# One rate in a planner's estimate: loads and stores taken to follow each other at the closer spacing throughout

## The chip, the cores and the metric

The kernel runs on one core of a Trainium2 chip. The metric is the device time of one execution in microseconds, here the median of three runs. TensorE (PE) multiplies matrices, with weight loads (PEld) beside it; VectorE (DVE), ScalarE (ACT) and GpSimd (POOL) do the rest, and SyncE (SP) issues nearly all DMAs. Each engine works through its own instructions in the order in which the program has them, and waits on semaphores for the others.

## The reference

One inference step of a two-layer streaming encoder, for a prompt of 2048 frames and a running stream of 32 frames, model width 1024, all in float32. Layer 0 is sliding-window attention (16 heads of 64, ALiBi, sinks), layer 1 a gated DeltaNet (8 heads of 128), each with a SiLU gate, a residual add and RMSNorm around it:

```
hp = rmsnorm(xp, norm_g[i]);  hs = rmsnorm(xs, norm_g[i])
layer 0: q, k, v, gate = split(h @ w_in);  o = sink_attention(q, k, v)
         y = (o * silu(gate)) @ w_out
layer 1: qkv, z, b, a = split(h @ w_in);   qkv = silu(causal_conv(qkv))
         o, s = gated_delta_chunked(l2norm(q), l2norm(k), v, g, beta, s0, 64)
         y = (rmsnorm(o) * silu(z)) @ w_out
xp = xp + yp;  xs = xs + ys
y_prompt = rmsnorm(xp, final_norm_g);  y_sample = rmsnorm(xs, final_norm_g)
```

Also returned are the newest K/V rows, the last rows before the convolution and the delta-rule states.

## The kernel before

**Tiles and stages.** Activations lie with features on the 128 partitions. The tokens are cut into four slabs of 512 (`SLABS`); the 32 sample frames ride on slab 1, which is therefore 544 wide and is multiplied in two groups of 272 columns. The attention layer runs over the four slabs, then the DeltaNet layer over the four slabs. Per slab a layer is a row of *blocks*: one block is one 1024x128 piece of a weight matrix against the slab. An attention slab has 20 input blocks and 8 output blocks (`wa`, `wao`), a delta slab 33 and 8 (`wd`, `wdo`).

**A block.** Each weight is split into a high and a low float32r part (tiles `wh`), and so are the activations (`hk`); a block is 8 x 3 matmuls (high by high, high by low, low by high) into one PSUM bank. Banks for blocks (`pj`) are two, used in turn (`BANKS`), so the bank of one block must have been emptied before the block after the next can start. In an output block (`out_blocks`) the emptying is one DVE addition, `xr <- pj, xr`, which adds the residual; ACT then squares it (`sq`), DVE sums the squares (`acc`), and a DMA stores it (`xsx1`).

**Weights.** In the attention layer a weight half of 256 KB is loaded to `wr` (3 buffers), ACT casts it to the high part (`wh <- wr`) and DVE subtracts to get the low part (`wh <- wr, wh`). There are 6 `wh` buffers; a block uses 4. Meanwhile `keep_ahead` does the same splitting for all 41 weights of the DeltaNet layer, in 82 halves, and writes the parts to DRAM: load `pr` (2 buffers), ACT cast `ph <- pr` (1 buffer), store, DVE subtraction `pr <- pr, ph`, store. The DeltaNet layer then loads its `wh` ready split (`wh <- xswwd`).

**Order.** The program is first generated in one order (classes `Kern`, `Estimate`) and only recorded. `Order.flush` then plans it anew, once after the attention layer and once at the end: a list scheduler that, with estimated durations, always takes the instruction that can start first, by rank among those ready on an engine. What it emits is the order in which each engine has to work. All instructions are recorded through one helper, so that every row of the profile has line L185. The planner counts DMAs on one shared channel, in ns:

```
self.free[e] = now + 60
self.dma = max(now + 1500, self.dma) + op.cost * (self.CLOSE if now < self.START else 1)
op.ends = {"dma": self.dma + 500}
```

`op.cost` is bytes / 250, thus 1049 for 256 KB. `CLOSE` is 0.7, which makes it 734 for 256 KB (250 and 357 bytes per ns). `START` is 25000: by the planner's own clock, the first 25 us. What needs a load, or the buffer of a store, can't stand in the order ahead of what the planner thinks starts before that DMA has landed.

Of the kernel before, what the change touches and what calls it, by code (L numbers as in the profile page):

```python
# [211 lines left out]
class Order:  # L212
# [2 lines left out]

    ENGINES = ("tensor", "vector", "scalar", "gpsimd", "sync")

    START, EARLY, CLOSE = 25000, 5000, 0.7

    EVAC, CHAIN = 400, 600  # L220
# [92 lines left out]
    def flush(self):  # L313

        overs = []
        for p in self.places.values():
            if p.old and p.over is None:
                p.over = Op(None)
                overs.append(p.over)
                for o in p.old.ops:  # L320
                    self.link(o, p.over)
                for o in {id(o): o for o in p.ops}.values():
                    self.link(p.over, o)
                    if o.gang:
                        self.link(p.over, o.gang)
        self.wait = {e: [] for e in self.ENGINES}
        ready = {e: [] for e in self.ENGINES}
        for o in [o for o in overs + self.ops if o.left == 0]:
            self.settle(o)
        while any(self.wait.values()) or any(ready.values()):  # L330
            when = {e: max(self.free[e], 0.0 if ready[e] else self.wait[e][0][0]) for e in self.ENGINES if ready[e] or self.wait[e]}
            e = min(when, key=when.get)
            now = when[e]
            while self.wait[e] and self.wait[e][0][0] <= now:
                _, rank, o = heapq.heappop(self.wait[e])
                heapq.heappush(ready[e], (rank, o))
            _, op = heapq.heappop(ready[e])
            op.call()
            if op.dma:
                self.free[e] = now + 60  # L340
                self.dma = max(now + 1500, self.dma) + op.cost * (self.CLOSE if now < self.START else 1)
                op.ends = {"dma": self.dma + 500}
            else:
                self.free[e] = now + op.cost
                op.ends = {e: self.free[e]}
            op.start = now
            self.finish(op)
        assert all(o.done for o in self.ops)
        self.ops = []
# [1903 lines left out]
```

## Time and profile before

| | |
|---|---|
| runs | 2346.01, 2347.42, 2352.44 us; median 2347.42 |
| profiled execution | 2349.7 us, of which span of the core 2347.9 us |
| PE busy | 2243.8 us (96%), weight loads 1842.6 (78%) |
| DVE, ACT, POOL busy | 1724.0 (73%), 1262.7 (54%), 467.8 (20%) |
| mean granted clock of PE | 0.98 |
| DMA | 382.75 MB, mean 163 GB/s |

The attention layer takes the first 915 us or so, the DeltaNet layer the rest; the splitting ahead ends at about 617 us. PE is busy nearly all the time; it is idle for 104 us in all, and its clock is at half in some stretches.

### The profile page before, as it was taken

The page shows a single profiled execution, that of the slowest core. Times are in us where ns is not written, and L with a number is a line of the kernel's source. Part 1 is how long each engine was busy: PE and PEld are TensorE (multiplying, and loading weights), DVE is VectorE, ACT ScalarE, POOL GpSimd, SP SyncE. Part 2 cuts the span into 40 slices and gives each one's busy share as a digit, 9 for nine tenths or more (in the row PEclk, how much of TensorE's full clock was granted, in tenths as well). Part 3 has the DMA queues.
Part 4 walks back from the last instruction along what each step waited for, and adds up shares of the span by engine and source line. Part 5 has one row for each costly group of instructions (what it writes and reads, how often), then busy time and mean ns, then how long its engine had stood idle before and what let it go on. Part 6 is the DMA issues. An engine that isn't in the chain of part 4 may idle for free.

```text
span 2347.9 us, 44428 instructions
## 1 busy us (share of the span) xinstructions
PE 2243.8 (96%) x14759; PEld 1842.6 (78%) x14759; DVE 1724.0 (73%) x5330; ACT 1262.7 (54%) x3792; POOL 467.8 (20%) x738
## 2 busy tenths in 40 slices
PE   8999999989999999999999999989999999999997
PEld 6777899877777777777788788867798777777776
DVE  7785667757665565688987677888886888786876
ACT  6664566546554553556566355465644465535533
POOL 0120000301110001222233031231313222122222
PEclk9999999999999999999999999999999999999998
DMA  8567655765443226544533673433457634476442
GB/s 272 190 203 231 219 187 183 222 220 193 153 138 112 66 64 203 180 133 127 173 95 112 207 240 102 133 115 125 149 177 226 188 117 137 139 225 206 153 139 68
DMA packets 222832, 382.75 MB, mean 163 GB/s; under 512 B 29922, under 2 KB 45194, under 8 KB 222602
## 3 DMA queue, kind: packets, MB, share of 16 engines
q1 hardware_dynamic: 220154, 377.75, 50.4%
q8 instruction: 116, 1.90, 0.3%
q10 hardware_dynamic: 2448, 2.16, 0.3%
q14 instruction: 114, 0.93, 0.1%
HBM read 311.63 MB, written 68.19 MB: 162 GB/s over the span
## 4 chain that ended last, share of the span: by engine, by line
PE 66%; DVE 22%; ACT 6%; issue 3%; DMA 1%; POOL 1%; SPq 0%; DVEq 0%; ACTq 0%; POOLq 0%
PE pj L185 47%; PE tb L185 7%; PE ta L185 6%; PE tc L185 4%; DVE cy L185 4%; DVE sub L185 3%; DVE tl L185 3%; ACT ta L185 2%; DVE ml L185 1%; DVE md L185 1%; DVE r L185 1%; PE ms L185 1%; ACT kd L185 1%; DVE st L185 1%; DVE kq L185 1%
## 5 line engine op out<-in xcount | busy, mean ns | idle before, releaser
L185 PE MATMUL pj<-hk,wh 128*128 128x512 f32 (+1 forms) x8184 | 1770.5, 363 | 34.0 <-DVE xr L185 16.3
L185 PEld LDWEIGHTS pj<-hk,wh 128*128 128x128 f32 x8184 | 1326.5, 191 | 246.4 <-issue 29.2
L185 DVE SCALAR_TENSOR_TENSOR cy<-cx,cw,cy 128x512 f32<-128x512 f32 x360 | 230.5, 651 | 45.7 <-ACT cy L185 40.9
L185 DVE TENSOR_TENSOR wh<-wr,wh 128x512 fp32r<-128x512 f32 x224 | 159.1, 712 | 139.5 <-ACT wh L185 129.4
L185 ACT CAST wh<-wr 128x512 fp32r<-128x512 f32 x224 | 138.0, 618 | 203.2 <-PE pj L185 174.0
L185 ACT ACTIVATE qs<-tb,egq 64x128 f32<-64x128 f32 x264 | 95.7, 362 | 90.5 <-DVE r L185 79.6
L185 POOL TENSOR_TENSOR hk<-of,hk 128x256 fp32r<-128x256 f32 (+1 forms) x72 | 53.4, 742 | 444.8 <-ACT hk L185 439.2
L185 ACT ACTIVATE s<-s,mx 128x256 f32<-128x256 f32 (+1 forms) x272 | 132.0, 487 | 7.5 <-DVE mx L185 7.2
L185 DVE TENSOR_TENSOR sub<-ml,tl 128x60 f32<-128x60 f32 (+24 forms) x527 | 125.8, 239 | 10.2
L185 ACT ACTIVATE cx<-cy 128x512 f32<-128x512 f32 (+1 forms) x96 | 61.1, 636 | 130.4 <-DVE cy L185 95.7
L185 DVE TENSOR_TENSOR tl<-tl,sub 128x60 f32<-128x60 f32 (+24 forms) x527 | 123.0, 233 | 10.1
L185 DVE CUSTOM_DVE_ANT_0 s<-ta,bias 128x256 f32<-128x256 f32 (+1 forms) x272 | 96.2, 404 | 25.6 <-PE ta L185 25.5
L185 DVE SCALAR_TENSOR_TENSOR r<-tb,nbk,vb 64x128 f32<-64x128 f32 x264 | 91.7, 348 | 29.8 <-PE tb L185 25.3
L185 ACT ACTIVATE qs<-o 128x128 f32<-128x128 f32 x132 | 40.7, 308 | 132.2 <-DVE o L185 126.8
L185 ACT COPY cx<-pj 128x512 f32<-128x512 f32 (+2 forms) x149 | 64.1, 445 | 77.8 <-PE pj L185 66.0
L185 PE MATMUL tb<-st,kq 128*128 128x128 f32 x512 | 95.0, 287 | 5.5 <-DVE st L185 5.0
L185 PEld LDWEIGHTS tb<-st,kq 128*128 128x128 f32 x512 | 82.7, 194 | 20.4 <-DVE st L185 12.3
L185 DVE SCALAR_TENSOR_TENSOR st<-st,egl,tc 128x128 f32<-128x128 f32 x128 | 44.3, 346 | 59.4 <-PE tc L185 56.9
L185 ACT COPY pt<-tb 128x512 f32<-128x512 f32 (+2 forms) x144 | 70.6, 528 | 26.4 <-PE tb L185 26.1
L185 DVE TENSOR_SCALAR s<-s,den 128x256 f32<-128x256 f32 (+1 forms) x272 | 81.7, 352 | 1.1
L185 PE MATMUL tc<-pt,vt 128*64 128x128 f32 (+2 forms) x1056 | 79.7, 279 | 1.1 <-DVE of L185 0.6
L185 POOL TENSOR_TENSOR so<-so,mhalf 128x4 f32<-128x4 f32 x33 | 36.8, 1114 | 216.4 <-DVE so L185 188.6
(242 smaller groups left out, 3447.8 us busy)
## 6 DMA issues: line engine op xcount, KB each, us to landing
wh<-xswwd SPq DMA_DIRECT2D x528, 256.0 KB, 2.9
wr<-in_wa SPq DMA_DIRECT2D x160, 256.0 KB, 3.3
wh<-xswwdo SPq DMA_DIRECT2D x112, 256.0 KB, 3.0
pr<-in_wd SPq DMA_DIRECT2D x66, 256.0 KB, 3.4
xswwd<-ph SPq DMA_DIRECT2D x66, 256.0 KB, 3.6
xswwd<-pr SPq DMA_DIRECT2D x66, 256.0 KB, 3.0
wr<-in_wao SPq DMA_DIRECT2D x64, 256.0 KB, 2.9
xa<-in_x SPq DMA_DIRECT2D x48, 256.0 KB, 4.0
```

The source lines that it names most:

```text
L185: self.order.add(Op(self.name, lambda: call(*args, **kw), cost, op == "dma_start"), ins, outs)
```

## The change

The planner's factor `CLOSE` holds for all DMAs and no more for those of the first 25 us alone. Nothing else changes: the same instructions with the same operands and buffers are recorded in the same order, and what the planner makes of them differs.

```
-                self.dma = max(now + 1500, self.dma) + op.cost * (self.CLOSE if now < self.START else 1)
+                self.dma = max(now + 1500, self.dma) + op.cost * self.CLOSE
```

The number `START` stays in use in `Order.add`, unchanged. The emitted order changes soon after the first blocks. On PE, ACT and DVE it is the same, or nearly, from where the splitting ahead ends to the end of the attention layer, and on all engines in the last delta slab.

DVE in the output blocks of slab 0 of the attention layer, before (`xr` empties the bank of a block, `wh` is a low weight part, `pr` a low part of the splitting ahead; the last number of a name counts tiles in the order of generation):

```order
L185 TENSOR_TENSOR wh_546_682<-wr_538_672,wh_545_681 128x512
L185 TENSOR_TENSOR xr_520_652<-pj_532_664,xr_520_652 128x512
L185 TENSOR_TENSOR acc_522_654<-acc_522_654,sq_542_676 128x512
L185 TENSOR_TENSOR wh_548_684<-wr_539_673,wh_547_683 128x512
L185 TENSOR_TENSOR pr_646_796<-pr_646_796,ph_680_832 128x512
L185 TENSOR_TENSOR wh_557_695<-wr_549_685,wh_556_694 128x512
L185 TENSOR_TENSOR wh_559_697<-wr_550_686,wh_558_696 128x512
L185 TENSOR_TENSOR xr_531_663<-pj_541_675,xr_531_663 128x512
```

The same place now:

```order
L185 TENSOR_TENSOR xr_520_652<-pj_532_664,xr_520_652 128x512
L185 TENSOR_TENSOR wh_546_682<-wr_538_672,wh_545_681 128x512
L185 TENSOR_TENSOR acc_522_654<-acc_522_654,sq_542_676 128x512
L185 TENSOR_TENSOR wh_548_684<-wr_539_673,wh_547_683 128x512
L185 TENSOR_TENSOR pr_797_957<-pr_797_957,ph_822_984 128x512
L185 TENSOR_TENSOR xr_531_663<-pj_541_675,xr_531_663 128x512
L185 TENSOR_TENSOR wh_557_695<-wr_549_685,wh_556_694 128x512
```

The emptying `xr_531` stood behind the low parts 557 and 559 and now stands ahead of both; and the splitting ahead, which had its tile `pr_646` here, has its tile `pr_797`.

DVE in the output blocks of slab 1 (two groups of 272 columns, so two emptyings a block), before:

```order
L185 TENSOR_TENSOR wh_1202_1396<-wr_1192_1385,wh_1201_1395 128x512
L185 TENSOR_TENSOR wh_1210_1406<-wr_1203_1397,wh_1209_1405 128x512
L185 TENSOR_TENSOR xr_1181_1373<-pj_1194_1387,xr_1181_1373 128x272
L185 TENSOR_TENSOR xr_1181_1373<-pj_1197_1391,xr_1181_1373 128x272
L185 TENSOR_TENSOR acc_1161_1351<-acc_1161_1351,sq_1207_1402 128x544
```

and now:

```order
L185 TENSOR_TENSOR xr_1181_1373<-pj_1194_1387,xr_1181_1373 128x272
L185 TENSOR_TENSOR wh_1202_1396<-wr_1192_1385,wh_1201_1395 128x512
L185 TENSOR_TENSOR xr_1181_1373<-pj_1197_1391,xr_1181_1373 128x272
L185 TENSOR_TENSOR wh_1210_1406<-wr_1203_1397,wh_1209_1405 128x512
L185 TENSOR_TENSOR pr_1715_1959<-pr_1715_1959,ph_1727_1973 128x512
```

Each emptying has moved ahead of the low part that it stood behind.

PE in delta slab 1 (`ta <- tq, mo` is a small product of the inverse, which waits for DVE; `pj` are blocks), before:

```order
L185 MATMUL pj_3449_12439<-hk_2881_11871,wh_3415_12405 128x272
L185 MATMUL pj_3449_12439<-hk_2881_11871,wh_3416_12406 128x272
L185 MATMUL pj_3449_12439<-hk_2884_11874,wh_3415_12405 128x272 x2
L185 MATMUL ta_3436_12426<-tq_3425_12415,mo_3321_12311 32x32
L185 MATMUL ta_3437_12427<-tq_3425_12415,mo_3321_12311 32x32
```

and now:

```order
L185 MATMUL pj_3469_12459<-hk_2884_11874,wh_3432_12422 128x272 x2
L185 MATMUL pj_3469_12459<-hk_2884_11874,wh_3433_12423 128x272
L185 MATMUL pj_3469_12459<-hk_2892_11882,wh_3452_12442 128x272 x2
L185 MATMUL ta_3436_12426<-tq_3425_12415,mo_3321_12311 32x32
L185 MATMUL ta_3437_12427<-tq_3425_12415,mo_3321_12311 32x32
```

The small products stand one block later: behind the second group of the block that follows.

## Rows read from the trace of the kernel before

**Rows 1.** The page: the span, and the busy time of PE.

```profile
span 2347.9 us, 44428 instructions
PE 2243.8 (96%) x14759; PEld 1842.6 (78%) x14759; DVE 1724.0 (73%) x5330; ACT 1262.7 (54%) x3792; POOL 467.8 (20%) x738
```

**Rows 2.** Windows by stage: PE, PEld, DVE, ACT, POOL busy; PE clock; DMA share; GB/s.

```profile
25.00:620.00 595.00, 574.40 (x4051) 483.67 (x4049) 411.88 (x1269) 348.34 (x933) 72.21 (x83) 0.99 0.64 208
620.00:915.00 295.00, 292.62 (x1714) 226.72 (x1714) 181.10 (x538) 152.47 (x397) 29.44 (x33) 1.00 0.33 105
915.00:1990.00 1075.00, 1027.85 (x6997) 858.10 (x6996) 851.18 (x2712) 582.34 (x1912) 280.70 (x495) 0.98 0.49 154
1990.00:2348.00 358.00, 330.58 (x1935) 259.69 (x1933) 264.79 (x789) 164.40 (x529) 83.63 (x120) 0.94 0.49 156
```

**Rows 3.** Waits of PE from 25 to 650 us: total us, times, longest.

```profile
PE pj L185 <- DVE xr L185: 15.9, 9, 1.9
PE pj L185 <- ACT hk L185: 1.8, 2, 1.6
```

**Rows 4.** Timeline of DVE, output blocks of slab 0: start, duration, idle before.

```profile
199.25 0.69 DVE L185 TENSOR_TENSOR xr<-pj,xr 128x512 f32<-128x512 f32 x1 [1.65 <-PE pj L185]
199.85 0.68 DVE L185 TENSOR_TENSOR wh<-wr,wh 128x512 fp32r<-128x512 f32 x1
...
204.79 0.69 DVE L185 TENSOR_TENSOR xr<-pj,xr 128x512 f32<-128x512 f32 x1 [1.67 <-PE pj L185]
```

**Rows 5.** Timeline of all engines, some blocks later.

```profile
226.79 0.62 ACT L185 CAST wh<-wr 128x512 fp32r<-128x512 f32 x1 [1.87 <-PE pj L185]
227.44 0.69 DVE L185 TENSOR_TENSOR wh<-wr,wh 128x512 fp32r<-128x512 f32 x1 [1.80 <-ACT wh L185]
228.05 0.68 DVE L185 TENSOR_TENSOR xr<-pj,xr 128x512 f32<-128x512 f32 x1
...
228.88 5.84 PE L185 MATMUL pj<-hk,wh 128*128 128x512 f32 x24 [1.94 <-DVE xr L185]
...
235.82 0.68 DVE L185 TENSOR_TENSOR xr<-pj,xr 128x512 f32<-128x512 f32 x1
```

**Rows 6.** Timeline of PE in the output blocks of slab 1.

```profile
475.31 6.22 PE L185 MATMUL pj<-hk,wh 128*128 128x272 f32 x48 [1.80 <-DVE xr L185]
```

**Rows 7.** Windows, PE alone: busy, clock, DMA share, GB/s.

```profile
196.00:227.00 31.00, 30.94 (x134) 1.00 0.82 273
227.00:248.00 21.00, 15.30 (x65) 0.92 0.65 203
238.00:241.40 3.40, 3.40 (x10) 0.50 0.62 204
465.00:505.00 40.00, 31.02 (x207) 0.91 0.68 220
484.00:497.40 13.40, 11.60 (x69) 0.75 0.70 225
```

**Rows 8.** DMA issues from 25 to 300 us: count, KB each, median us to landing.

```profile
wr<-in_wa SPq DMA_DIRECT2D x51, 256.0 KB, 3.7
...
pr<-in_wd SPq DMA_DIRECT2D x36, 256.0 KB, 3.3
xa<-in_x SPq DMA_DIRECT2D x26, 256.0 KB, 4.7
```

**Rows 9.** DMA issues of the whole run, from the page.

```profile
wh<-xswwd SPq DMA_DIRECT2D x528, 256.0 KB, 2.9
```

**Rows 10.** The splitting's DVE work (`pr`) in a window: busy, clock, share, GB/s.

```profile
25.00:620.00 595.00, 58.29 (x82) 0.99 0.64 208
```

**Rows 11.** Waits for DMAs from 25 to 650 us, the one of ACT on the splitting.

```profile
ACT ph L185 <- DMA xswwd<-ph: 2.1, 3, 1.3
```

**Rows 12.** Waits of PE from 915 us to the end.

```profile
PE tb L185 <- DVE r L185: 13.5, 12, 3.8
PE ta L185 <- DVE tq L185: 7.0, 10, 2.1
```

## Prediction

> **What bounds the kernel now.** I read the page first. PE is busy for 2243.8 of 2347.9 us [rows 1], so the kernel is bound by TensorE, and a new order can only move the other 104 us and the stretches at half clock. The windows by stage say where these are [rows 2]: 20.6 us idle from 25 to 620 us (595.00 - 574.40), 2.4 us from 620 to 915, 47.2 us from 915 to 1990 and 27.4 us in the last slab and the end. The stage from 25 to 620 us is the one in which the weights of the second layer are split ahead; there the DMA share is 0.64, and right behind it, with that work done, 0.33.
>
> Next the waits of PE in that stage [rows 3]: of its idle time 15.9 us, in nine waits of up to 1.9 us, ended with the DVE addition `xr`, which empties a block's bank. Nothing else there comes near: the next is 1.8 us. The timeline shows what it is. Early in slab 0's output blocks an `xr` runs at 199.25 and the next at 204.79 us, each directly after its block ended, with a low weight part behind it [rows 4]; a block takes 5.54 us and PE is busy 30.94 of 31 us [rows 7]. Some blocks later `xr` stands behind a low part that itself waited 1.80 us for ACT; it starts at 228.05, PE gets its bank only then and sits idle for 1.94 us [rows 5]; the next `xr` follows at 235.82, so that a block takes 7.77 us. DVE was not short of time (busy for 411.88 of 595 us [rows 2]), it had an instruction in front that was waiting. Slab 1 has the same, 1.80 us before a block of 6.22 us [rows 6].
>
> The planner put it there. It counts 1049 ns on one channel for each 256 KB, 250 GB/s; the stage moves 208 on average and 273 in the output blocks [rows 2, 7], so in its books the channel is full, loads land late, and what hangs on them slides behind what does not. The chip was not late: the cast in that place waits for PE to free a buffer (at 226.79 [rows 5]), and ACT waited for the splitting's stores only 2.1 us in all [rows 11].
>
> **The change, part by part.** No instruction is added or removed; every edit is a move.
>
> *The emptyings move ahead of the low parts (slabs 0 and 1).* The order quoted for the change has in every output block of both slabs the pattern of the early blocks of slab 0, one emptying ahead of the low parts. Nine waits, 15.9 us, go [rows 3]. What would be late next is the weight part that now runs behind `xr`, 0.69 us later; in the blocks from 196 to 227 us it stood so, and PE lost 0.06 us in 31 [rows 7]. So I take -15.9, with 0 as the other end if the bank is late for another reason.
>
> *The clock.* The granted clock was 1.00 (2.4 GHz) from 196 to 227 us and 0.50 (1.2 GHz) from 238.0 to 241.4, amid three of these waits (PE busy 15.30 of 21 us from 227 to 248); from 484.0 to 497.4 it was 0.75 on average, again amid them [rows 7]. At half clock half the work is lost: 3.4 x 0.50 = 1.7 us and 13.4 x 0.25 = 3.4 us, together 5.1. Without the waits I take these as gone: -5.1, bounds -5.1 and 0.
>
> *The splitting ahead runs earlier.* Its 82 halves, 58.29 us of DVE [rows 10] and as many casts, are the same work in other places; in the output blocks of slab 0 DVE is then five halves further on (tile 797 for 646). It is hidden under PE as before, since DVE and ACT are busy 69% and 59% of the stage. Its price is the DMA queue. One output block of slab 0 with one half in it moves 7 transfers of 256 KB (two weight halves, residual in, sum out, one load and two stores of the splitting), 1.835 MB, at 5.54 us 331 GB/s. The row from 196 to 227 us gives 273 GB/s at a share of 0.82 [rows 7], 333 at a full share: with nine halves in eight blocks, 15.5 MB, it takes 46.5 us for 44.3 us of PE work, 2.2 us over. For the loads of the next slab's statistics, which land after 4.7 us at this load where weights take 3.7 [rows 8], I add a like amount, as they stand ahead of other work on ACT and DVE. I take +5 in all. The bounds are 0 (at a share of 0.82 PE lost nothing [rows 7]) and +21 (the queue gives all of the gain back).
> The Trainium skill (DMA: Bandwidth & Descriptors, Specifications) puts the limit of memory for one core at about 358 GB/s, almost the planner's new 357; by that, 331 fits and the 2.2 us fall away, which would make the sum 2 us less. The trace of this case has no stretch above the 333 worked out here, so the measured one decides.
>
> *The DeltaNet layer.* Weight loads there land after 2.9 us [rows 9], between the 2.73 us (1500 + 734 + 500) that the planner will now count for a transfer alone and the 3.05 (1500 + 1049 + 500) that it counted. Blocks move forward on PE and the small products of inverse and chain backward, by up to one block, as in the place quoted, where PE then has 6 us more work (a block of 48 matmuls [rows 6]) in front of a product that waited for DVE. Such waits are the largest there: 13.5 us for `r`, 7.0 for `tq` [rows 12]. But a chain that runs later is later for its own next step too, and at the end of the slab it is work that stands alone. No row tells the sign. I take 0, bounds -15 and +15, a third of the 47 us idle from 915 to 1990 us [rows 2].
>
> *The sum* for the profiled execution, 2349.7 us with 1.8 us around the span: 2349.7 - 15.9 - 5.1 + 5 = 2333.7. The median of the runs is 2.3 us lower (2347.42), so I forecast 2332 there (2331.4, rounded up).
>
> **The rivals.**
> *The queue sets the pace (slower).* The splitting's cast `ph` has one buffer, so it waits for its own store, and ACT waits with it, in order; behind it stand the casts of the weights PE needs. Before, the planner's late landings kept these apart (2.1 us of such waits [rows 11]). If the landings rise by a microsecond, as from the 3.7 of weights to the 4.7 of `xa` [rows 8], each of 82 halves can hold ACT for 1 us; with a third of it reaching PE, since ACT is 59% busy [rows 2], that is +27, against which perhaps 15 of the 21 us remain: 2347.4 + 12 = 2359. It decides once the DMA share from 25 us to the splitting's end comes near the 0.82 that only the output blocks have now. Against it: at 0.82 PE lost nothing [rows 7].
> The Trainium skill (DMA: Bandwidth & Descriptors, Latency and other measured facts) has the latency of memory go from 0.2 us on average to 2 us at high load, which speaks for this rival. In this trace a transfer's landing grew from 2.9 to 3.7 and 4.7 us between the lighter and the fuller stage [rows 8, 9], a part of it.
> *The gain is spent in the second layer, or does not come (no change).* The chain's later place costs 12 of the 15 us at the three slab ends, or the emptyings are early in the order and still behind a splitting step that waits for its load. 2332 + 12 = 2344.
> *The second layer gains too (faster still).* The waits for `tq` and `r` shrink behind more block work: -15, 2317. For it speaks that the new count is no worse than the old beside 2.9 us; against it that DVE is 79% busy there [rows 2] and its own chain stays as long.
>
> **How the numbers follow.** Forecast 58%, with its own range 2324 to 2341; queue 12%; no change 18%; faster still 12%. A measurement of this kernel can tell about 0.3%, 7 us, from no change, so "within" is 2340.4 to 2354.5 us. Faster: 0.92 of the forecast's 58, all of the 12, a fifth of the 18: 0.69. Within: the rest of the forecast's and most of the 18: 0.18. Slower: 0.13. The range from 2316 to 2354 leaves out half of the faster case and nearly all of the slower one.
>
> **What would show it.** In the profile after, PE's waits for `xr` before 650 us should be under 3 us; the window of slab 0's output blocks should show PE over 98% busy at clock 1.00; the splitting should end some 80 us earlier than at 617 us (it is a fifth faster by the places quoted), with a DMA share near 0.70 up to there; idle time of PE from 915 us on should be within 15 us of the 75 before. I am wrong if ACT or DVE wait more than 20 us for the splitting's DMAs, or if PE's idle time in the second layer grows by more than what the first one gave.

## The result and the profile after

The changed kernel takes 2319.70 us (median; 2317.96 to 2324.83) where the kernel before, run beside it, takes 2347.41 (2346.01 to 2352.44). The ratio is 0.9872, with a 95% interval from 0.9854 to 0.9891: 27.7 us less. I had forecast 2332 with 2316 to 2354; the time lies inside that, but below the 2324 to 2341 of the forecast itself: the gain is nearly twice the 15 us that I had worked out, and close to the rival "the second layer gains too" (2317).

The page of the kernel after, its span and the busy times, against [rows 1]:

```profile
span 2316.7 us, 44447 instructions
PE 2227.7 (96%) x14759; PEld 1829.2 (79%) x14759; DVE 1716.8 (74%) x5330; ACT 1262.1 (54%) x3792; POOL 471.6 (20%) x738
```

The span is 31.2 us shorter. PE does the same 14759 matmuls in 16.1 us less, so 16.1 us of the 31.2 are clock (its mean went from 0.980 to 0.987), and the other 15.1 us are idle time of PE (104.1 to 89.0). That split is the profiled execution's: the other four of the changed kernel were granted 0.983 or 0.984 at nearly the same times, so the clock's share of the gain is likely smaller there.

To see where, I cut both traces at the same three matmuls of the program: the end of the attention layer, the last matmul of a block shortly ahead of the hand-over from delta slab 0 to slab 1, and one after slab 1. Windows of the kernel before (start and end; length; PE, PEld, DVE, ACT, POOL busy; clock; DMA share; GB/s):

```profile
25.00:907.00 882.00, 859.02 (x5728) 703.94 (x5727) 588.98 (x1802) 498.32 (x1324) 101.64 (x116) 0.99 0.54 174
907.00:1298.00 391.00, 377.80 (x2436) 309.74 (x2435) 303.17 (x963) 214.03 (x687) 110.72 (x193) 0.99 0.45 144
1298.00:1717.00 419.00, 394.28 (x2872) 340.27 (x2871) 332.34 (x1089) 225.38 (x768) 104.75 (x198) 0.97 0.48 152
1717.00:2347.00 630.00, 594.36 (x3660) 474.23 (x3659) 484.45 (x1454) 309.83 (x989) 148.87 (x224) 0.96 0.51 162
```

And of the kernel after:

```profile
25.00:895.00 870.00, 856.30 (x5726) 701.92 (x5725) 589.91 (x1801) 498.47 (x1323) 100.90 (x116) 1.00 0.55 177
895.00:1289.00 394.00, 378.18 (x2434) 310.21 (x2433) 300.55 (x952) 214.02 (x688) 114.21 (x193) 0.98 0.45 143
1289.00:1695.00 406.00, 386.21 (x2880) 334.19 (x2879) 330.81 (x1098) 224.32 (x768) 107.56 (x198) 0.99 0.50 157
1695.00:2316.00 621.00, 588.55 (x3658) 468.27 (x3655) 480.40 (x1457) 310.02 (x989) 147.15 (x224) 0.98 0.52 164
```

Row by row: the attention layer is 12 us shorter (idle 22.98 to 13.70, busy 2.7 less); the stretch to slab 1 is 3 longer; delta slab 1 is 13 shorter (idle 24.72 to 19.79, busy 8.1 less); the rest is 9 shorter (idle 3.2, busy 5.8 less). The numbers of matmuls differ by a few, since small products stand on the other side of a cut.

In the attention layer the waits of PE from 25 to 650 us, against [rows 3], are now (total us, times, longest):

```profile
PE ms L185 <- DVE acc L185: 4.0, 2, 2.1
PE tb L185 <- DVE s L185: 3.5, 5, 1.4
PE pj L185 <- ACT wh L185: 1.2, 2, 0.7
```

No wait for `xr` is left. The timeline of PE, where [rows 5] had a wait of 1.94 us amid slab 0's output blocks, has all 192 of their matmuls (8 blocks of 24) in one row of 204 without a wait, and behind them a new wait, for the sum of squares (`acc`) that closes the slab's norm:

```profile
198.10 45.08 PE L185 MATMUL pj<-hk,wh 128*128 128x512 f32 x204
245.33 1.05 PE L185 MATMUL ms<-ones,acc 128*128 128x1 f32 x8 [2.15 <-DVE acc L185]
```

Windows of that stretch and of slab 1's end, against [rows 7], and of the splitting ahead up to its last store:

```profile
25.00:527.00 502.00, 491.25 (x3528) 418.73 (x3527) 365.94 (x1105) 305.46 (x813) 63.60 (x72) 0.99 0.72 236
...
198.00:244.00 46.00, 45.18 (x206) 37.00 (x204) 25.17 (x40) 18.80 (x33) 0.00 (x0) 1.00 0.91 299
490.20:497.10 6.90, 6.90 (x21) 5.61 (x21) 2.82 (x6) 2.36 (x4) 1.52 (x2) 0.51 1.02 349
```

PE is 98% busy in slab 0's output blocks at a DMA share of 0.91; at the end of slab 1 the clock still falls to half, for 6.9 us, right behind the second `acc` wait:

```profile
489.65 1.49 PE L185 MATMUL ms<-ones,acc 128*128 128x1 f32 x10 [1.81 <-DVE acc L185]
```

In the DeltaNet layer PE waits, against [rows 12] and, for the loads, 0.8 us before:

```profile
PE tb L185 <- DVE r L185: 15.6, 17, 3.2
PE pj L185 <- DMA wh<-xswwd: 7.3, 8, 1.7
PE ta L185 <- DVE tq L185: 6.0, 10, 1.9
```

The waits for the chain (`r`, `tq`) are 21.6 us, 20.5 before; the loads of weights cost more than before. So the gain there did not come from the waits that I had named for it.

### The profile page after: what moved, and what is told of

The parts are those of the page before. It is cut to its first block, busy times and chain, and to the rows that moved or that the text cites. A ratio compares the mean times of both kernels' runs of the same rounds, so it can differ in the third digit from the quotient of the medians.

```text
span 2316.7 us, 44447 instructions
## 1 busy us (share of the span) xinstructions
PE 2227.7 (96%) x14759; PEld 1829.2 (79%) x14759; DVE 1716.8 (74%) x5330; ACT 1262.1 (54%) x3792; POOL 471.6 (20%) x738
## 5 line engine op out<-in xcount | busy, mean ns | idle before, releaser
L185 DVE TENSOR_TENSOR pr<-pr,ph 128x512 fp32r<-128x512 f32 x82 | 57.2, 697 | 42.0 <-ACT ph L185 30.5
```

Source lines behind the costliest of these rows:

```text
L185: self.order.add(Op(self.name, lambda: call(*args, **kw), cost, op == "dma_start"), ins, outs)
```

## Experiments

All twelve were timed in five rounds against the kernel before. It ran there at 2351 to 2353 us (medians), some 5 us above the 2347 that the expectations were written for, so the ratio decides; the last column is the ratio times 2347.4. The edits below are shown in part; `...` marks what is left out of a line.

| kernel | median us | ratio | 95% interval | at 2347.4 |
|---|---|---|---|---|
| the change | 2319.70 | 0.9872 | 0.9854 to 0.9891 | 2317 |
| e1, attention layer only | 2338.66 | 0.9951 | 0.9933 to 0.9968 | 2336 |
| e2, DeltaNet layer only | 2337.51 | 0.9941 | 0.9927 to 0.9954 | 2334 |
| e3, output blocks only | 2337.14 | 0.9931 | 0.9915 to 0.9946 | 2331 |
| e4, a meaningless nudge | 2351.90 | 0.9999 | 0.9987 to 1.0011 | 2347 |
| e9, emptyings behind again | 2352.30 | 0.9995 | 0.9984 to 1.0006 | 2346 |
| e10, tanh ahead again | 2322.17 | 0.9857 | 0.9838 to 0.9875 | 2314 |
| e11, PE's order of before | 2351.31 | 0.9999 | 0.9987 to 1.0011 | 2347 |
| e12, PE's order of after alone | 2348.41 | 0.9985 | 0.9971 to 1.0000 | 2344 |
| e14, old spacing, early landing | 2333.13 | 0.9924 | 0.9906 to 0.9942 | 2330 |
| e5, 0.85 for 0.7 | 2321.42 | 0.9855 | 0.9839 to 0.9872 | 2313 |
| e7, 1700 for 1500 ns | 2310.79 | 0.9811 | 0.9794 to 0.9827 | 2303 |
| e13, e5 and e7 together | 2308.47 | 0.9817 | 0.9800 to 0.9835 | 2304 |

**The two layers apart (e1, e2).** `Order.flush` runs once per layer (a counter, `flushes`), so each can have the old or the new count.

```
-  ... op.cost * (self.CLOSE if now < self.START else 1)                       # before
+  op.cost * (self.CLOSE if self.flushes == 1 else 1)                          # e1
+  op.cost * (self.CLOSE if now < self.START or self.flushes == 2 else 1)      # e2
```

> The closer spacing holds for the planning of the whole attention layer and not for that of the DeltaNet layer, which is planned with the old count. Theory (two separate gains): the attention layer keeps its gain, the emptyings stand ahead of the low weight parts, PE's waits for xr before 650 us are under 1 us, and the layer ends 12 to 13 us earlier, as in the changed kernel; the DeltaNet layer takes what it took before. Time 2347.4 - 13 = 2334 us, plus or minus 3. Rival (all of the 28 us is one effect, the splitting's earlier end): about 2320.

> The closer spacing holds for the first 25 us and for the planning of the DeltaNet layer alone. Theory: the attention layer is as before (nine waits for xr, 15.9 us); the DeltaNet layer gains by its own order, mainly in its slab 1, where the two traces differ by 18 us between the same blocks. Time 2347.4 - 15 = 2332 us, plus or minus 4, and with the attention layer's gain the two add up to the 28 us. Rival (the second layer's gain is clock and chance of one execution): 2342 to 2350.

Each gives about half: -0.49% and -0.59%. Their product is 0.9892, the change's ratio 0.9872; with the intervals of both factors the two agree, so the layers add as far as these runs tell. I had the DeltaNet layer at nothing. Cut at the same matmuls, e1's stretch of delta slab 1 is as long as before (419 us), and e2's is 408:

```profile
1288.00:1707.00 419.00, 393.13 (x2871) 337.61 (x2869) 332.73 (x1089) 225.25 (x768) 105.40 (x198) 0.98 0.48 152
```

```profile
1301.00:1709.00 408.00, 390.06 (x2871) 336.87 (x2870) 330.36 (x1095) 224.30 (x768) 108.88 (x198) 0.97 0.50 156
```

The whole layer, from the end of the attention layer on, says what kind of time it is (length; PE busy; clock; DMA share; GB/s). First the kernel before and e1, with the old count there, then the change, e2 and e9 (an experiment below that has the new count in this layer):

```profile
907.00:2347.00 1440.00, 1366.43 (x8964) 0.97 0.49 154
895.00:2335.00 1440.00, 1364.07 (x8965) 0.97 0.49 154
```

```profile
895.00:2316.00 1421.00, 1352.94 (x8965) 0.98 0.50 156
910.00:2334.00 1424.00, 1359.24 (x8966) 0.98 0.50 156
927.00:2350.00 1423.00, 1356.52 (x8965) 0.98 0.49 156
```

With the new count the layer is 16 to 19 us shorter in each trace. PE's idle time falls from 73.6 and 75.9 us to 68.1, 64.8 and 66.5, and its busy time, for the same matmuls, by 5 to 14 us, which is clock. So both are part of the gain, in shares that differ from trace to trace.

**The attention layer's cause (e3, e9).** e3 counts the new spacing only while the planner's clock is in the output blocks of slabs 0 and 1 (and in the first 25 us); e9 is the change with one rule for the planner, that an emptying stays behind the first low part three blocks (slab 1: two) further on.

```
+  ... if now < self.START or 165000 <= now < 235000 or 375000 <= now < 470000 else 1   # e3
```

```
+  for e in kern.emptied.pop(self.src[1], []):              # e9, in Weights.split, after the first low part
+      kern.issue.link(kern.issue.ops[-1], e)
+  self.emptied.setdefault(f + (2 if slab[2] else 3), []).append(self.issue.ops[-1])   # in out_blocks
```

> The closer spacing holds for the first 25 us and, by the planner's clock, from 165 to 235 and from 375 to 470 us, which are the output blocks of slabs 0 and 1; elsewhere in both layers the old count. Theory: the emptyings' order alone makes the first layer's gain, 15 to 20 us (15.9 us of waits, and the half clock at 238 and 484 us with them), a little more than in the changed kernel, since the splitting is not run earlier elsewhere: time 2327 to 2333 us. Rival (the splitting's earlier end makes the gain, or the queue takes it back): 2340 or more.

> The changed kernel with one rule added for the planner alone: in the output blocks of attention slabs 0 and 1 the emptying of a block may not be ordered ahead of the first low part of a weight three blocks on (slab 0) or two blocks on (slab 1), where it stood before the change. Theory (the emptyings' place is the first layer's gain): PE waits for xr again, some nine to eleven times about 1.8 us, 16 to 20 us, a few us of half clock with them; 2334 to 2345 us, and the gain of delta slab 1 stays. Rival (the bank would be late anyway, or the splitting running earlier made the gain): xr waits under 6 us, 2317 to 2326 us.

e3 keeps all of the layer's gain (0.9931 to e1's 0.9951). e9 loses it and more. Waits of PE in e9 from 25 to 650 us, its first window and that of delta slab 1:

```profile
PE pj L185 <- DVE xr L185: 27.7, 13, 3.9
```

```profile
25.00:927.00 902.00, 864.23 (x5725) 707.74 (x5724) 589.28 (x1801) 499.26 (x1323) 100.69 (x116) 0.99 0.53 170
...
1317.00:1725.00 408.00, 390.38 (x2881) 337.57 (x2881) 331.17 (x1097) 223.89 (x768) 109.40 (x198) 0.97 0.49 157
```

The layer is 32 us longer than in the changed kernel (902 to 870), 24 of them idle time of PE, and the waits for `xr` are back at 27.7 us; delta slab 1 keeps its gain (408). The obvious rival is that the splitting's earlier end makes the gain. Its last store is issued at 527.30 us in the changed kernel, at 569.67 in e3 and at 515.58 in e9:

```profile
527.30 0.33 SPq L185 DMA_DIRECT2D xswwdo<-pr  x1
569.67 0.41 SPq L185 DMA_DIRECT2D xswwdo<-pr  x1
515.58 0.38 SPq L185 DMA_DIRECT2D xswwdo<-pr  x1
```

The kernel that ends it earliest has lost the gain, and the one that ends it 42 us later than the change keeps it. So the emptyings' place is shown as the cause, in both directions. The price in e9 was larger than the 16 to 20 us that I expected: more waits (13), longer ones (3.9), and 7.9 us more of busy time, which is clock. It is no measure of what the old order cost: e9 holds back every emptying of these blocks, also those that stood early before [rows 4], and its layer is 20 us longer than that of the kernel before (902 to 882).

**A control (e4).** A change of the planner's numbers that means nothing, 1490 for 1500 ns in the DeltaNet layer of the kernel before, asks whether any reordering there gains.

```
+  max(now + (1490 if self.flushes == 2 else 1500), self.dma)
```

> The kernel before, with the planner's fixed part of a DMA in the DeltaNet layer 10 ns shorter (1490 for 1500): a change without meaning that reorders a few hundred instructions. It measures what any reordering does. Theory (the second layer gains because the planner's channel is no longer full): 2347 plus or minus 3. Rival (that layer's time moves by 10 us and more with any reordering, and the gain is luck): outside 2340 to 2354.

It changes nothing (0.9999). So a new order as such does not give 14 us there; but by the expectation it moves a few hundred instructions only, and the control speaks for moves of that size.

**What in the DeltaNet layer (e10, e11, e12).** The trace showed a copy of the attention layer's pattern. In delta slab 1 of the kernel before, ACT had a tanh (`cx <- cy`) that waits for DVE's convolution in front of the next block's first emptying (`cx <- pj`), and PE waited for the bank. ACT, then PE:

```profile
1415.25 0.66 ACT L185 ACTIVATE cx<-cy 128x544 f32<-128x544 f32 x1 [6.68 <-DVE tl L185]
1415.82 0.37 ACT L185 COPY cx<-pj 128x272 f32<-128x272 f32 x1
```

```profile
1416.63 4.63 PE L185 MATMUL pj<-hk,wh 128*128 128x272 f32 x35 [1.97 <-ACT cy L185]
```

In the order of slab 1, 10 of 24 blocks had it so, and 3 of 24 after the change. e10 is the change with the seven tanh's that moved put in front again. e11 and e12 ask for PE's own order: the planner first plans the layer with one count without emitting, keeps TensorE's row, and plans again with the other count with that row fixed.

```
+  if x.tensor.name.startswith(BEHIND):     # e10: the seven tiles
+      self.behind("tanh", seq)             # links tanh -> first emptying of the next block
```

```
+  row = [o for o in self.plan(ops, 1, False) if o.engine == "tensor"]     # e11; e12 has self.CLOSE here
+  for x, y in zip(row, row[1:]): x.order.append(y); y.left += 1
+  self.plan(ops, self.CLOSE, True)                                        # e12 has 1 here
```

> The changed kernel with one rule added for the planner alone: in delta slab 1 the seven tanh's of ACT that the change moved behind the next block's first emptying have to stand ahead of it again, as before the change. Theory (ACT, held by a tanh that waits for DVE's convolution, empties the bank late): PE is idle for 8 to 15 us more between 1357 and 1608 us, in waits for ACT's cx or cy ahead of a block; 2328 to 2335 us, attention unchanged. Rival (blocks moving forward past the small products made the gain): 2317 to 2324 us.

> The changed kernel, but in the DeltaNet layer TensorE works in the order that the old count gives, while all other engines are planned with the new count around it. Theory (where PE's blocks stand against its small products makes the second layer's gain of 15 us): the gain there is gone, 2333 to 2342 us. Rival (the order on ACT, DVE and of the loads makes it): the gain stays, 2317 to 2326 us. A time in between, near 2329, would say that both are needed.

> The reverse: in the DeltaNet layer TensorE works in the changed kernel's order, while all other engines are planned with the old count around it. Theory (PE's own order makes the gain): 2317 to 2326 us, the wait for DeltaNet weights' loads still about 7 us. Rival (ACT, DVE and the loads): 2333 to 2342 us.

My theory on the tanh fell: e10 is as fast as the change (0.9857 and 0.9872, with intervals that overlap). Waits for its bank did come (PE from 1290 to 1620 us in e10), but of 2.8 us:

```profile
PE pj L185 <- ACT cx L185: 2.8, 2, 1.6
```

So did the theory on PE's order, and its rival with it. Either half of the new plan without the other loses the layer's gain and about as much again: both kernels are back, or nearly back, at the time before, though both have the new count in the attention layer. A row of PE that was made for one count waits for engines that were ordered by the other: PE is idle for 82 us in e11 and 85 us in e12 from the end of the attention layer on (893 to 2349 and 896 to 2341 us), where the kernel before has 73.6. The loads, for which I expected some 7 us of waits in e12, cost 1.1. PE's waits from 890 us on, e11 and e12:

```profile
PE tb L185 <- DVE r L185: 12.9, 14, 3.2
PE ta L185 <- DVE tq L185: 11.4, 7, 5.8
...
PE pj L185 <- ACT cy L185: 5.6, 8, 1.3
```

```profile
PE pj L185 <- ACT cy L185: 11.7, 11, 2.3
PE tb L185 <- DVE st L185: 10.0, 14, 1.3
PE pj L185 <- DVE hk L185: 9.3, 2, 9.0
```

A mixed plan has a cost of its own, so these two runs do not tell whose order makes the gain. I can't put it down to one engine.

**Which half of the count (e14).** The new count does two things: a load alone lands earlier in the books (2.73 for 3.05 us), and loads that follow each other land closer (734 for 1049 ns). e14 keeps the first and takes back the second in the DeltaNet layer.

```
+  max(now + (1500, 1185)[self.flushes - 1], self.dma) + op.cost * (self.CLOSE, 1)[self.flushes - 1]
```

> The changed kernel, but in the DeltaNet layer the planner counts the old spacing (1049 ns for a weight half) with a fixed part of 1185 for 1500 ns, so that a lone half lands in its books as early as in the changed kernel (2.73 us), and only loads that follow each other are counted at the old distance. Theory (the spacing of loads that follow each other makes the second layer's gain): that gain is lost, 2332 to 2341 us. Rival (the earlier landing of each single load makes it): the gain stays, 2316 to 2326 us.

The layer's gain is gone, or all but a few us of it: 0.9924, where e1 and e3, with the old count there, have 0.9951 and 0.9931. Delta slab 1 in e14, cut as above, takes 420 us (before 419, after 406):

```profile
1291.00:1711.00 420.00, 399.01 (x2887) 343.22 (x2885) 333.19 (x1090) 225.94 (x768) 105.67 (x198) 0.96 0.49 152
```

So it is the spacing that makes the gain, and not the earlier landing; e7 below, with the spacing and a later landing, keeps it. In e14's one trace the part that is missing is clock: over the whole layer PE's idle time is 66.4 us, as with the new count, and its busy time is as with the old one.

```profile
899.00:2334.00 1435.00, 1368.59 (x8965) 0.97 0.49 155
```

It may be the attention layer's cause again, in another place. Where slab 1 begins, the kernel before moves 231 GB/s, in books that hold 250:

```profile
1366.00:1415.00 49.00, 44.68 (x352) 41.78 (x350) 41.39 (x126) 23.53 (x85) 17.29 (x34) 1.00 0.71 231
```

That nearly full books are what put the instructions in the wrong order there is argued from e14 and this row, and no run prints the books themselves; which of the moved instructions cost the time and the clock stays open.

**Other numbers (e5, e7, e13).**

```
-  START, EARLY, CLOSE = 25000, 5000, 0.7
+  START, EARLY, CLOSE = 25000, 5000, 0.85                                           # e5
+  max(now + (1700 if self.flushes == 2 else 1500), self.dma) + ...                  # e7
+  max(now + (1500, 1700)[self.flushes - 1], self.dma) + op.cost * (0.85, 0.7)[self.flushes - 1]   # e13
```

> The changed kernel with 0.85 for 0.7 (294 bytes per ns in the planner's books). Theory (what matters is whether the planner's channel is full): 294 lies above the stage's mean and near or under the 300 to 330 that slab 0's output blocks move, so some emptyings fall behind again: PE waits for xr 2 to 10 us, 2322 to 2336 us. Rival (any number under 1 does as well as 0.7): xr waits under 1 us, 2316 to 2324 us.

> The changed kernel, but the planner's fixed part of a DMA is 1700 ns for 1500 in the second layer, so that a lone weight half is booked at 2.93 us, as the 2.9 us that the trace shows, and not 2.73. Theory: a low booked landing is what made PE wait for the DeltaNet weights' loads (0.8 us before, 7.3 us after the change); with 2.93 these waits fall to about 3 us, 2313 to 2319 us. Rival: the loads wait for the queue or their buffers and not for the order; waits stay at 7 us, 2317 to 2324 us.

> The changed kernel with two numbers moved, each as it did best alone: 0.85 for 0.7 in the attention layer (its trace ended that layer 18 us ahead of the kernel before, the changed kernel 12), and 1700 for 1500 ns as the fixed part in the DeltaNet layer (25 us gained there, the changed kernel 17). Theory (the layers add): 2298 to 2310 us, PE waits for DeltaNet loads near 4 us, no half clock before 900 us. Rival (the differences between these kernels are chance of where the clock falls): 2311 to 2323 us, as the two kernels alone.

e5 is the same as the change within the intervals, so 0.85 does as well as 0.7, and by its time the rival won: 294 GB/s in the books are enough, beside the 231 of slab 1 before and the 299 that slab 0's output blocks moved after. Its trace has six waits for `xr`, of 1.5 us in all, a little over the rival's 1 us and under the theory's 2 to 10, and an attention layer at full clock that is 5 us shorter than that of the change (865 for 870); the runs don't tell these 5 us from nothing.

```profile
25.00:890.00 865.00, 855.08 (x5731) 700.82 (x5730) 589.77 (x1802) 498.93 (x1324) 102.67 (x116) 1.00 0.55 178
```

e7 is faster than the change, with intervals that don't meet. PE's waits for weights in e7 from 890 us on:

```profile
PE pj L185 <- DMA wh<-xswwd: 4.1, 6, 1.4
```

They fell from 7.3 to 4.1 us, near what I expected (about 3), and delta slab 1 takes 403 us for 406. The books now say 2.93 us for a lone weight half, and the median landing was 2.9 [rows 9]. But the time, 2303 on the scale of 2347.4, is 10 us below the 2313 to 2319 of the theory: 3.2 us of load waits do not explain 14 us, and where the rest comes from is open. Of the kernels that the runs tell apart it is the fastest. e13 lies within e7's interval, so its extra step in the attention layer is not shown to give anything.

## Why the prediction was right, and where not

**What bounds the kernel, and the emptyings (-15.9): right.** All nine waits for `xr` are gone, PE is 98% busy in slab 0's output blocks, and e3 and e9 show the cause from both sides.

**What would be late next: wrong, and the size met by luck.** I named the weight part behind `xr`. What came late was the sum of squares at each slab's end (two waits, 4.0 us) and, with the work further on, small waits of the attention itself (`s` 3.5 for 1.1 us). With these the layer's idle time fell by 9.3 us and not by 15.9; the 6.6 us between are near the +5 that I had booked under the queue, for another reason. That is luck.

**The clock (-5.1): too large.** Half-clock stretches went on behind the new wait (6.9 us at 0.51). PE's busy time in the layer fell by 2.7 us. With -9.3 of idle time that is -12 in the trace, against the -16 that the three terms had for this layer; by ratio e1 gives -11.5, e3 -16.

**The splitting earlier, and the queue: the limit and the sign to watch wrong.** It ended at 527.6 us (I had said 80 us before 617), with a DMA share of 0.72 up to there (0.70). ACT did wait for the splitting's DMAs, and far over the 20 us that I had given as the sign of being wrong (total us, times, longest, from 25 to 650 us):

```profile
ACT ph L185 <- DMA pr<-in_wd: 18.5, 10, 3.5
ACT ph L185 <- DMA pr<-in_wdo: 14.7, 7, 3.3
ACT ph L185 <- DMA xswwd<-ph: 14.4, 11, 2.2
```

These 47.6 us reached PE hardly at all: its waits for ACT's weight casts are 1.2 us. ACT is 61% busy up to 527 us (305.46 of 502), and the six `wh` buffers lay between it and PE. Of the three rows only the last, 14.4 us, is what that rival named, the cast behind its own store; the other two wait for loads. So the rival in which the queue sets the pace had its mechanism in part and not its price, and the sign that I had chosen for it was a bad one: a wait on an engine with slack says nothing until a wait of PE follows.

The limit of 333 GB/s, worked out from a mean over 31 us, was none. The row at 490 us has 349, and the kernel before moves more near its start, against my sentence that its trace has no stretch above 333 (window; PE busy; clock; DMA share; GB/s):

```profile
7.00:14.00 7.00, 7.00 (x19) 1.00 1.04 398
```

So the 2.2 us over, and the like amount that I added for late statistics, rest on a limit that no run shows; slab 0's output blocks moved 299 GB/s in the changed kernel with PE 98% busy.
The Trainium skill (DMA: Bandwidth & Descriptors, Specifications) has about 358 GB/s as the limit of memory for one core; the 398 of this row lies above that too, so here the measurement decides.

**The DeltaNet layer (0, bounds ±15): the step that failed.** It gave -14 by ratio (e2: 0.59% of 2347) and -19 in the trace, at the edge of my bounds and beyond. I had weighed loads (2.9 us beside 2.73 and 3.05) and PE's waits for the chain, and those changed little. What I did not do was to read the stage slab by slab as I had read the attention layer: [rows 2] give 154 GB/s from 915 to 1990 us, far from the 250 of the books, but the first 49 us of slab 1's work move 231. The reason that I gave for the first layer, full books, may well hold in this place too (argued, not shown), and e14 shows that without the spacing there is no gain. I had also left the clock out of this layer's term. In this pair of traces most of the gain is clock: over the three stretches PE's busy time fell by 13.5 us (8.1 of them in that of slab 1) and its idle time by 5.5; e2 and e9 have 7 and 10 us of busy time and 9 and 7 of idle time. Idle time from 895 us on, 68 us, stayed within my 15 us of the 75, so that sign could not have shown this gain.

**The chances.** I gave the case that came 12%. Its mechanism was the waits for `tq` and `r`, which did not shrink; what the runs show, the spacing, was not among my rivals. The time lies in the range of 2316 to 2354 because the range was drawn wide enough for a rival whose mechanism did not come true, and that is luck.

## What to carry to other kernels

When a planner's estimate is wrong, look for every stretch in which its books are near full, window by window and not by stage: there it can let instructions slide behind ones that wait (shown here for the attention layer, argued for the other). An emptying of a bank that stands behind an instruction that waits costs TensorE that wait, here 15.9 us in nine waits, and can cost clock behind it. And bring an estimate to the measured number in both its parts, spacing and landing: with the closer spacing alone the books had a lone load down at 2.73 us where 2.9 is measured, and PE waited 7.3 us for loads; with 2.93 it waited 4.1, and the kernel was faster (e7).

## What the runs showed of the hardware

The same kind of wait at the same place in the program does not always cost the clock: behind the `acc` wait of slab 0 (2.15 us) the clock stayed at 1.00 in the changed kernel, and behind one of 1.36 us in e7 it fell to half for a while. The window around it after, then the wait and the window in e7:

```profile
244.00:252.00 8.00, 6.67 (x54) 6.67 (x55) 5.07 (x10) 3.52 (x7) 1.39 (x1) 1.00 0.99 317
```

```profile
247.37 1.05 PE L185 MATMUL ms<-ones,acc 128*128 128x1 f32 x8 [1.36 <-DVE acc L185]
```

```profile
245.00:256.00 11.00, 9.64 (x66) 9.42 (x65) 6.77 (x13) 4.86 (x10) 1.39 (x1) 0.84 0.96 331
```

The five executions of the changed kernel were granted 0.983 to 0.987 on average; 0.004 of PE's 2228 us is about 9 us (an estimate). So single stretches of half clock in one profiled execution are no basis for a term of 3 to 5 us, and a difference of that size between two traces can be chance.

The landing of weight loads did not grow with the queue: `wr` took 3.7 us at the median from 25 to 300 us before [rows 8], and 3.6 after, with more of the splitting in that stretch. The splitting's own transfers did: its loads took 3.3 us before [rows 8] and 3.6 after, the stores of its low parts (`xswwd<-pr`) 2.7 before and 3.4 after.

```profile
wr<-in_wa SPq DMA_DIRECT2D x52, 256.0 KB, 3.6
xswwd<-pr SPq DMA_DIRECT2D x45, 256.0 KB, 3.4
pr<-in_wd SPq DMA_DIRECT2D x44, 256.0 KB, 3.6
```
